# Moving small sums, scalings and a column sum between engines in a two-layer attention kernel, with the whole program in a new order

## The chip, the cores and the metric

The kernel runs on one core of a Trainium2 chip. The time is device microseconds of one execution, the median of several. Products run on TensorE (PE, its weight loads PEld), elementwise work on VectorE (DVE), ScalarE (ACT) and GpSimd (POOL); SyncE (SP) issues nearly all transfers.

## The reference

There are 256 positions of 1024 numbers, in f32, and two layers. Every layer is normalised, shifted, scaled and gated by sums over a conditioning vector `c`:

```
c_act = silu(c)
for layer in range(2):
    ada = c_act @ w_ada[layer] + b_ada[layer]     # 1024 -> 3072
    shift, scale, gate = split(ada, 3)
    h = rms_norm(x, norm_g[layer]) * (1 + scale) + shift
    x = x + gate * mixer(h)
x = rms_norm(x, ...)
```

Layer 0's mixer projects `h` to two groups of heads, A (8 heads, a window of 128 with sinks) and B (8 heads, three branches: compressed, selected, window), multiplies their outputs by `silu` of further projections, and projects back to 1024. Layer 1's mixer has 16 heads; at 256 positions it is causal attention.

## The kernel before, in words

Big products are made of rounded halves. `split` makes `hi`, the f32 number rounded to TensorE's fast format (a cast on ScalarE, `whi`), and `lo`, what is left of it (a difference on VectorE, `wlo`); `mm3` then runs three products, hi·hi, hi·lo and lo·hi. `hhi` and `hlo` are such halves of a layer's input `h`, `ghi` and `glo` those of the gated attention output.

The sums over `c` take three forms. `start_sums` makes layer 0's shift and scale for 2, 2, 2 and 2 columns of 128 (`START`), four sums side by side in one bank (`ps_m`), partly as products with `cz` (the vector `c_act`, one column repeated 32 times) and, in the later groups, partly as a running sum `acc` on VectorE that a product with `ones` then adds over the partitions; the weights lie in buffers that are free so early (`qT`, `gate`, `late`). Its first group has no running sum. `ada_jobs` and `ada_wide` make the later sums, among them layer 1's shift and scale: weight tiles of two rows of 128 go to VectorE, each row one `SCALAR_TENSOR_TENSOR acc<-raw,cz,acc`, save the last `SS_PE` tiles, which `ada_shift_scale` gives to TensorE as products `ps_m<-raw,cz`, 32 columns of weights by 256. `ada_gate` makes a layer's gate: the running sum `acc` is added over the partitions by a matrix of ones, in f32, or, where `GATE_R` says so, as `hi` and `lo` with a rounded matrix of ones (`ones_r`).

`attn_four` does the softmax of four heads for layer 0: scores, maximum (`mn`, VectorE), exponential (ScalarE), then each score tile is scaled by its reciprocal sum `rc`, transposed on TensorE (`ps_pt<-ta,late`) and copied out by ScalarE. Query rows come in two halves: t=0 has tiles of 128x128, t=1 of 128x256. `ON_ACT` says which scalings run on ScalarE.

Nothing runs in the order of the code. Each operation is recorded in a plan, and `ORDER`, a list of some 3,000 operation numbers, says in which order they are issued; it sets the order on all engines and of the transfers, which stand in one queue. So every row of the profile has the same line, 244, and is told by its tiles: `raw` are weights as loaded, `t` scratch tiles, `xs` the residual, `parts` the sums of squares, `late` and `bigA` score tiles, `shs` the finished shift and scale. `WARM` products of ones run ahead of the first data. At the layer boundary the last quarter of layer 0's output (`ps_s` in the rows below) is gated (`t<-ps_s,gate`) and added to `xs`; `xs` is normalised, transposed (`ps_pj<-ta,t`, `ps_o<-ta,t`), scaled and shifted (`t<-ps_pj,shs`), and rounded (`hhi`).

Of the kernel before, what the change touches and what calls it, by code (L numbers as in the profile page):

```python
# [24 lines left out]
GATE_R = (0, 1)  # L25
HV = 4
SS_PE = {0: 0, 4: 2}
SPL = (1024, 1024, 512, 512)
LAST = ((("a", 0, 384), ("v", 384, 1024)), (("a", 0, 192), ("a", 192, 384), ("f", 768, 1024), ("v", 384, 768)))
ON_ACT = ((0, 0, 1), (0, 1, 1), (1, 0, 1), (1, 1, 1))  # L30
# [225 lines left out]
def tile_trunk(  # L256
# [23 lines left out]
    plan = Plan(tc.nc)  # L280
# [433 lines left out]
    def start_sums(g, n, d, w):  # L714
# [10 lines left out]
        for q in range(4):  # L725
# [3 lines left out]
            if d:  # L729
                tq.insert(len(tq) - 1, (ones[:, 0:32], av[:, s_, cs]))  # L730
            terms.append(tq)
        ids = []
        for m in range(max(len(tq) for tq in terms)):
            for q, tq in enumerate(terms):
                if m < len(tq):
                    ids.append(T.matmul(
# [649 lines left out]
```

## Time and profile before

| | before |
|---|---|
| median of 3 runs | 294.93 us (294.6 to 295.61) |
| profiled run | 295.04 us |
| its span, first to last instruction | 293.33 us |
| granted TensorE clock, mean | 0.995 |
| transfers | 71.72 MB, 245 GB/s over the span |

In the rows of the timeline and the groups stand the engine, the line, the operation, `out<-in` by tile names, the shape and the count. In the groups the two numbers behind the bar are busy microseconds and mean nanoseconds of one, and behind the second bar the idle time of the engine just before them. In the timeline the first two numbers are start and length. Products of f32 leave two records each, products of rounded halves one.

### The profile page before, as it was taken

The numbers are of one execution on the slowest core, as the hardware profiler recorded it, in microseconds if no ns is written. First come the engines' busy times: TensorE is split into PE (matmuls) and PEld (weight loads), VectorE is DVE, ScalarE is ACT, GpSimd is POOL, SyncE is SP. The second block draws the span as 40 slices with busy tenths as digits, with TensorE's granted clock in tenths as the row PEclk, the third lists the DMA queues.
The fourth block names the chain that finished last, engine by engine and source line by source line (L and its number), as shares of the span: only waits on it lengthen the run. The fifth ranks groups of instructions, "written<-read, shape, count | busy, mean of one in ns | idle before, by whom it ended". The sixth has DMA issues, their size and how long they took to land.

```text
span 293.3 us, 6197 instructions
## 1 busy us (share of the span) xinstructions
PE 285.4 (97%) x2293; PEld 246.6 (84%) x2293; DVE 252.8 (86%) x629; ACT 188.5 (64%) x480; POOL 8.1 (3%) x33
## 2 busy tenths in 40 slices
PE   8999999999999999999999999999999999999991
PEld 8888788897897888777767899998899999887891
DVE  0497797999999999999889759779978999899884
ACT  4456256895998899994457863366658368584531
POOL 3000000000000000000020000000000000000021
PEclk9999999999999999999999999999999999999998
DMA  7999999999969942769986954569489709502003
GB/s 262 381 365 380 384 380 349 344 349 322 389 233 359 351 147 74 249 234 332 333 256 206 349 167 135 191 242 283 146 258 291 244 0 335 205 36 72 1 3 142
DMA packets 48431, 71.72 MB, mean 245 GB/s; under 512 B 2490, under 2 KB 33938, under 8 KB 48402
## 3 DMA queue, kind: packets, MB, share of 16 engines
q1 hardware_dynamic: 47906, 70.93, 70.6%
q8 instruction: 18, 0.29, 0.4%
q10 hardware_dynamic: 496, 0.41, 0.4%
q14 instruction: 11, 0.09, 0.1%
HBM read 70.28 MB, written 1.05 MB: 243 GB/s over the span
## 4 chain that ended last, share of the span: by engine, by line
PE 82%; DMA 11%; DVE 1%; ACT 1%; issue 1%; POOL 1%; POOLq 0%; DVEq 0%; ACTq 0%
PE ps_pj L244 53%; PE ps_s L244 10%; PE ps_o L244 7%; PE ps_pt L244 7%; PE ps_m L244 5%; DMA gate<-in_w_ada_dram 3%; DMA late<-in_w_ada_dram 3%; DMA raw<-in_w_in_even_dram 3%; DMA qT<-in_w_ada_dram 2%; DMA xs<-in_x_dram 1%; DVE wlo L244 1%; ACT t L244 1%; ACT whi L244 1%; POOL parts L244 1%; DVE t L244 0%
## 5 line engine op out<-in xcount | busy, mean ns | idle before, releaser
L244 ACT CAST whi<-raw 128x512 fp32r<-128x512 f32 (+2 forms) x116 | 71.8, 658 | 27.1 <-PE ps_pj L244 16.5
L244 DVE TENSOR_TENSOR wlo<-raw,whi 128x512 fp32r<-128x512 f32 (+2 forms) x100 | 71.3, 740 | 7.3 <-ACT whi L244 6.6
L244 PE MATMUL ps_pj<-hlo,whi 128*128 128x256 f32 x256 | 70.0, 288 | 0.0
L244 PE MATMUL ps_pj<-hhi,whi 128*128 128x256 f32 x256 | 69.9, 289 | 0.0
L244 PE MATMUL ps_pj<-hhi,wlo 128*128 128x256 f32 x256 | 68.3, 284 | 0.0
L244 PEld LDWEIGHTS ps_pj<-hhi,whi 128*128 128x128 f32 x256 | 46.7, 188 | 1.6 <-issue 0.7
L244 PEld LDWEIGHTS ps_pj<-hlo,whi 128*128 128x128 f32 x256 | 47.1, 189 | 0.8 <-issue 0.7
L244 PEld LDWEIGHTS ps_pj<-hhi,wlo 128*128 128x128 f32 x256 | 46.7, 189 | 0.3
L244 ACT ACTIVATE late<-late,mn 128x128 f32<-128x128 f32 (+1 forms) x58 | 26.0, 450 | 9.2 <-DVE mn L244 9.1
L244 DVE SCALAR_TENSOR_TENSOR acc<-raw,cz,acc 128x1024 f32<-128x1024 f32 x24 | 30.6, 1276 | 0.1
L244 PE MATMUL ps_pj<-whi,hlo 128*128 128x512 f32 (+2 forms) x72 | 25.6, 373 | 0.0
L244 PE MATMUL ps_pj<-wlo,hhi 128*128 128x512 f32 (+2 forms) x72 | 25.5, 372 | 0.0
L244 DVE SCALAR_TENSOR_TENSOR wlo<-raw,whi 128x512 fp32r<-128x512 f32 x32 | 21.1, 686 | 4.5 <-ACT whi L244 4.4
L244 PE MATMUL ps_pj<-whi,hhi 128*128 128x512 f32 (+2 forms) x72 | 24.8, 373 | 0.0
L244 PE MATMUL ps_pj<-wlo,ghi 128*128 128x512 f32 (+1 forms) x56 | 20.6, 371 | 0.0
L244 PE MATMUL ps_pj<-whi,ghi 128*128 128x512 f32 (+1 forms) x56 | 20.6, 371 | 0.0
L244 PE MATMUL ps_pj<-whi,glo 128*128 128x512 f32 (+1 forms) x56 | 20.4, 367 | 0.0
L244 PE MATMUL ps_pt<-ta,late 128*128 128x128 f32 x87 | 19.6, 275 | 0.0
L244 ACT COPY late<-ps_pt 128x384 f32<-128x384 f32 (+1 forms) x29 | 14.0, 483 | 7.9 <-PE ps_pt L244 7.6
L244 PEld LDWEIGHTS ps_pj<-whi,hhi 128*128 128x128 f32 x72 | 13.4, 188 | 2.5 <-ACT hhi L244 0.7
L244 PEld LDWEIGHTS ps_pj<-whi,hlo 128*128 128x128 f32 x72 | 13.6, 188 | 2.0 <-issue 0.2
L244 PEld LDWEIGHTS ps_pj<-wlo,hhi 128*128 128x128 f32 x72 | 13.4, 189 | 1.6
(243 smaller groups left out, 591.0 us busy)
## 6 DMA issues: line engine op xcount, KB each, us to landing
raw<-in_w_in_odd_dram SPq DMA_DIRECT2D x16, 1024.0 KB, 5.7
raw<-in_w_ada_dram SPq DMA_DIRECT2D x8, 1024.0 KB, 8.3
raw<-in_w_ada_dram SPq DMA_DIRECT2D x16, 512.0 KB, 6.3
raw<-in_w_in_even_dram SPq DMA_DIRECT2D x5, 1024.0 KB, 7.9
raw<-in_w_in_even_dram SPq DMA_DIRECT2D x7, 652.0 KB, 7.6
late<-in_w_ada_dram SPq DMA_DIRECT2D x16, 256.0 KB, 6.8
raw<-in_w_out_even_dram SPq DMA_DIRECT2D x4, 1024.0 KB, 5.8
raw<-in_w_out_odd_dram SPq DMA_DIRECT2D x4, 1024.0 KB, 8.7
```

Source lines behind the costliest of these rows:

```text
L244: self.ops.append(dict(key=eng.key, deps=deps, fn=lambda: getattr(real, name)(*args, **kw)))
```

## The change

Four constants or loops change, and the order list.

```
-GATE_R = (0, 1)
+GATE_R = (1, 1)
-SS_PE = {0: 0, 4: 2}
+SS_PE = {0: 0, 4: 1}
-ON_ACT = ((0, 0, 1), (0, 1, 1), (1, 0, 1), (1, 1, 1))
+ON_ACT = tuple((n, i, t) for n in range(2) for i in range(2) for t in range(2))
...
         ids = []
-        for m in range(max(len(tq) for tq in terms)):
-            for q, tq in enumerate(terms):
-                if m < len(tq):
+        size = 4 if d else 2
+        for o in range(0, 4, size):
+            for m in range(max(len(tq) for tq in terms)):
+                for q in range(o, o + size):
+                    tq = terms[q]
+                    if m >= len(tq):
+                        continue
                     ids.append(T.matmul(
...
-        for o in range(0, len(ids), 4):
-            plan.group(ids[o : o + 4])
+        for o in range(0, len(ids), size):
+            plan.group(ids[o : o + size])
...
 ORDER = [int(i) for i in """
-5 0 45 4 9 685 2 3 6 10 37 7 1 85 11 40 38 35 86 12 87 13 14 15 16 17 70 18 88 19 89 20 71 21 72 22 55 23 46 41 39 42 47
+0 4 2 3 1 5 44 45 9 6 35 37 10 7 42 85 11 86 12 87 13 14 15 16 70 88 48 17 49 8 71 18 89 50 55 36 72 90 41 52 46 73 91
...
```

Layer 0's gate is summed as rounded halves too (a cast, a difference and four products in place of two f32 products). In layer 1's second half of shift and scale one weight tile instead of two stays on TensorE; the other goes to the running sum. All of layer 0's scalings stand on ScalarE, 24 of 128x128 more than before. The first sums of layer 0 run the two shift sums to their end and then the two scale sums, instead of four side by side. The order list is new throughout; it has 3,000 operations instead of 3,002.

TensorE at the start of the program, before (`ones` are the products ahead of the data, `crow` and `rows` transposes of `c` and of small vectors, `t_91` and `t_89` transposes of the input, and `qT` the weights of the first shift and scale sums):

```order
L244 MATMUL ps_o_68<-ones 128x128 x15
L244 MATMUL ps_pt_85<-ta,crow 128x8
L244 MATMUL ps_o_68<-ones 128x128 x5
L244 MATMUL ps_pj_95<-ta,t_91 128x128
...
L244 MATMUL ps_s_93<-ta,t_89 128x128 x3
L244 MATMUL ps_m_107<-qT_98,cz 32x128 x2
L244 MATMUL ps_m_107<-qT_100,cz 32x128 x2
L244 MATMUL ps_m_107<-qT_98,cz 32x128 x2
L244 MATMUL ps_m_107<-qT_100,cz 32x128 x2
```

And now:

```order
L244 MATMUL ps_o_68<-ones 128x128 x8
L244 MATMUL ps_pt_85<-ta,crow 128x8
L244 MATMUL ps_o_68<-ones 128x128 x2
L244 MATMUL ps_pt_85<-ta,rows 128x24
L244 MATMUL ps_o_68<-ones 128x128 x5
L244 MATMUL ps_pj_95<-ta,t_91 128x128
L244 MATMUL ps_pj_94<-ta,t_91 128x128
L244 MATMUL ps_pj_95<-ta,t_91 128x128
L244 MATMUL ps_m_107<-qT_98,cz 32x128 x4
```

The transposes of `c` and of the small vectors stand ahead of fewer ones-products, and the first sums stand between the transposes of the input, two side by side.

TensorE at the layer boundary, before: the last product of layer 0's output, four transposes of layer 1's input, the sums of layer 1's shift and scale, and layer 1's first product (`whi,hhi`).

```order
L244 MATMUL ps_s_93<-whi_111,glo 128x512
L244 MATMUL ps_pj_96<-ta,t_88 128x128 x4
L244 MATMUL ps_o_68<-ta,t_88 128x128
L244 MATMUL ps_m_107<-acc_106,ones 32x256 x4
L244 MATMUL ps_m_107<-raw_105,cz 32x256 x8
L244 MATMUL ps_m_107<-raw_103,cz 32x256 x8
L244 MATMUL ps_pj_94<-whi_112,hhi 128x512
```

And now:

```order
L244 MATMUL ps_s_93<-whi_112,glo 128x512
L244 MATMUL ps_pj_96<-ta,t_88 128x128 x4
L244 MATMUL ps_m_107<-acc_106,ones 32x256 x4
L244 MATMUL ps_m_107<-raw_103,cz 32x256 x8
L244 MATMUL ps_o_68<-ta,t_88 128x128 x2
L244 MATMUL ps_pj_94<-whi_113,hhi 128x512
```

Eight products of the sums are gone, and one transpose more stands ahead of layer 1's first product.

ScalarE in layer 0's attention, before (the first scalings by `rc`, between exponentials `late,den<-late,mn` and `es`, and copies out of the banks):

```order
L244 ACTIVATE late,den_127<-late,mn_124 128x128
L244 COPY qT_99<-ps_pt_85 128x2x128
L244 ACTIVATE late<-late,rc_130 128x256
L244 ACTIVATE h_140<-ps_m_107 128x128
L244 ACTIVATE es_134<-mn_124,snk 128x2
L244 ACTIVATE late,den_127<-late,mn_124 128x128
L244 ACTIVATE late,den_127<-late,mn_124 128x256
L244 ACTIVATE h_140<-h_140 128x128
L244 ACTIVATE late<-late,rc_130 128x256
```

And now:

```order
L244 ACTIVATE late,den_127<-late,mn_124 128x128
L244 ACTIVATE late<-late,rc_130 128x128
L244 ACTIVATE late<-late,rc_130 128x256
L244 COPY qT_99<-ps_pt_85 128x2x128
L244 ACTIVATE late<-late,rc_130 128x256 x2
L244 ACTIVATE h_140<-ps_m_107 128x128
L244 ACTIVATE late<-late,rc_130 128x128
L244 ACTIVATE late<-late,rc_130 128x256
L244 ACTIVATE late<-late,rc_130 128x128
```

The scalings of 128x128 stand beside those of 128x256. The cast of the gate's sum, `whi_112<-acc_106`, is placed in the same stretch, further down.

230 rows, old and new, of the table ORDER are left out of this document.

## The prediction

> **What bounds the kernel now.** I read the head of the profile's page first: busy shares, then the shares of the chain that ended last.
>
> ```profile
> PE 285.4 (97%) x2293; PEld 246.6 (84%) x2293; DVE 252.8 (86%) x629; ACT 188.5 (64%) x480; POOL 8.1 (3%) x33
> PE 82%; DMA 11%; DVE 1%; ACT 1%; issue 1%; POOL 1%; POOLq 0%; DVEq 0%; ACTq 0%
> ```
>
> TensorE is on the chain for 82% of the span, transfers for 11%. Where they change places is in the chain in order of time (start, length, what) and in TensorE's own timeline.
>
> ```profile
> 0.80 3.35 DMA xs<-in_x_dram
> 4.16 7.62 DMA gate<-in_w_ada_dram
> 11.79 7.51 DMA late<-in_w_ada_dram
> 19.32 7.42 DMA raw<-in_w_in_even_dram
> 26.75 6.09 DMA qT<-in_w_ada_dram
> ...
> 31.82 0.58 PE L244 MATMUL ps_pj<-whi,hhi 128*128 128x408 f32 x2
> 32.89 0.64 PE L244 MATMUL ps_m<-qT,cz 128*32 128x128 f32 x16 [0.50 <-DMA qT<-in_w_ada_dram]
> ```
>
> Up to 32.89 us an unbroken row of transfers sets the time: the third group of layer 0's shift and scale sums cannot start before its weights land at 26.75 + 6.09 = 32.84. TensorE is out of work half a microsecond earlier. From then on, look at whole stretches (columns: us, then busy time and instructions of PE, PEld, DVE, ACT, POOL, the granted clock, DMA share).
>
> ```profile
> core 0: us, PE busy (x) PEld busy (x) DVE busy (x) ACT busy (x) POOL busy (x), PEclk, DMA share, GB/s
> 14.74:32.89 18.15, 17.65 (x127) 14.65 (x125) 15.76 (x32) 9.24 (x21) 0.00 (x0) 1.00 1.07 373
> 70.00:139.00 69.00, 69.00 (x600) 55.05 (x597) 68.71 (x216) 59.43 (x178) 0.00 (x0) 1.00 0.76 268
> 139.00:150.56 11.56, 11.56 (x50) 8.88 (x50) 9.37 (x18) 5.64 (x10) 1.18 (x3) 1.00 0.98 335
> 160.00:287.05 127.05, 127.05 (x1019) 115.45 (x1016) 110.38 (x256) 75.11 (x182) 1.75 (x4) 1.00 0.52 176
> 287.05:293.33 6.28, 0.00 (x1) 0.00 (x0) 1.92 (x6) 0.80 (x2) 0.55 (x1) 0.77 0.37 136
> ```
>
> The first row has the only pause, 0.50 us, and its transfers are at their limit. In the next three TensorE is busy without a break. That is layer 0's attention (70 to 139), its output projection, and layer 1. In the projection 50 products of 512 columns take 11.56 us, 0.231 each, the same step as elsewhere, so nothing is hidden in "busy" there. The last row is a tail of 6.28 us that no product enters. So what counts is TensorE's own work after 32.89, the pause before it, and whether VectorE (68.71 of 69.00 us!) and ScalarE (59.43) still keep up in the attention.
>
> **The change part by part.** *Opening: pairs and other order.* The same transfers stand ahead of the third group's weights, save a few tiny ones that change places, so the pin near 32.84 stays. In the new order, counted row by row by columns, 0.44 us more product work stands ahead of the third group's sums and 0.87 us more ahead of those behind them. Work put into the pause is work not done later: at least 0 (if the pin moves later by as much), at most the pause: 0.50 by the row, or 0.70 if the last two products of 408 columns, from 31.82, take 0.231 × 408/512 = 0.184 each and end at 32.19. I take 0.5 saved, near the 0.44. Fewer ones-products ahead of the constants and sums in pairs instead of fours lie before 14.74; each sum is still two products of the same width in one bank, and the copy behind them waits for all.
>
> ```profile
> 11.05 1.18 PE L244 MATMUL ps_m<-qT,cz 128*32 128x128 f32 x34
> 13.10 0.27 ACT L244 COPY asb<-ps_m 128x128 f32<-128x128 f32 x1 [3.83 <-PE ps_m L244]
> ```
>
> If all of those sums came twice as slowly (1.18 us more), 0.7 would be covered by the pause and 0.5 would show. I cost them at nothing.
>
> *Layer 0's gate by rounded halves.* TensorE loses two f32 products of 512 columns (two records each) and gets four rounded ones. The timeline gives the old ones with their followers; the groups by shape give the rest.
>
> ```profile
> 100.85 1.02 PE L244 MATMUL ps_m<-acc,ones 128*128 128x512 f32 x2
> 101.80 1.08 PE L244 MATMUL ps_o<-bigA,vb 128*64 128x256 f32 x9
> ...
> 103.74 1.02 PE L244 MATMUL ps_m<-acc,ones 128*128 128x512 f32 x2
> 104.70 0.93 PE L244 MATMUL ps_s<-late,qT 64*128 64x128 f32 x8
> ...
> L244 PE MATMUL ps_m<-acc,ones 128*128 128x512 f32 x4 | 2.0, 592 | 0.0
> L244 PE MATMUL ps_m<-whi,ones_r 128*128 128x512 f32 x2 | 0.8, 392 | 0.0
> L244 PE MATMUL ps_m<-wlo,ones_r 128*128 128x512 f32 x2 | 0.8, 392 | 0.0
> L244 ACT CAST whi<-acc 128x1024 fp32r<-128x1024 f32 x1 | 1.0, 1049 | 0.0
> L244 DVE TENSOR_TENSOR wlo<-acc,whi 128x1024 fp32r<-128x1024 f32 x1 | 1.2, 1218 | 0.0
> ```
>
> Each old product holds TensorE 0.95 us (100.85 to 101.80, 103.74 to 104.70), together 1.91; four at 0.231 are 0.92. That saves 0.98. The groups' busy times, which count overlaps between neighbours, give 2.0 − 1.6 = 0.4. I take 0.9, since a follower's start tells more than a modelled end. For it ScalarE gets a cast of 1.05 and VectorE a difference of 1.22; they stand in the attention, where TensorE has other products.
>
> *Layer 1's sums.* A second weight tile of two goes to VectorE. TensorE loses half of 32 records, VectorE gets two sums of 1024 columns.
>
> ```profile
> L244 PE MATMUL ps_m<-raw,cz 128*32 128x256 f32 x32 | 1.9, 379 | 0.0
> L244 DVE SCALAR_TENSOR_TENSOR acc<-raw,cz,acc 128x1024 f32<-128x1024 f32 x24 | 30.6, 1276 | 0.1
> ...
> 150.33 0.39 PE L244 MATMUL ps_s<-whi,glo 128*128 128x512 f32 x1
> 151.71 1.91 PE L244 MATMUL ps_m<-raw,cz 128*32 128x256 f32 x32
> 153.55 0.50 PE L244 MATMUL ps_pj<-whi,hhi 128*128 128x512 f32 x1
> ...
> 151.02 0.68 DVE L244 TENSOR_TENSOR t<-ps_s,gate 128x512 f32<-128x512 f32 x1
> 151.94 0.68 DVE L244 TENSOR_TENSOR xs<-xs,t 128x512 f32<-128x512 f32 x1
> ...
> 153.03 0.41 ACT L244 CAST hhi<-t 128x256 fp32r<-128x256 f32 x1 [1.26 <-DVE t L244]
> ```
>
> That is 1.91/2 = 0.95 us less of TensorE and 2 × 1.276 = 2.55 more of VectorE. But look where the sums stand: they fill the layer boundary. While they run (151.71 to 153.55), VectorE gates the last part of layer 0's output (151.02), adds it to the residual (151.94) and makes two columns of layer 1's input, and ScalarE rounds them (153.03 to 153.44); only then can layer 1's first product start, 0.11 us later, at 153.55. That chain stays as it is in the new order. With 0.95 of the cover gone TensorE waits about as long; one or two transposes pulled in ahead are all that it keeps. I take 0.1 saved; the ends are 0 and 0.95.
>
> *Scalings to ScalarE.* Layer 0 has 24 scalings of 128x128 on VectorE, which go to ScalarE. The groups:
>
> ```profile
> L244 DVE TENSOR_SCALAR late<-late,rc 128x128 f32<-128x128 f32 x29 | 7.8, 277 | 0.0
> L244 ACT ACTIVATE late<-late,rc 128x256 f32<-128x256 f32 x15 | 7.4, 507 | 0.2
> L244 ACT ACTIVATE late<-late,mn 128x128 f32<-128x128 f32 x29 | 11.5, 396 | 3.5 <-DVE mn L244 3.5
> ```
>
> VectorE loses 24 × 0.277 = 6.6 us. For a scaling of 128 columns on ScalarE there is no row: it lies between 0.277 (VectorE's for the same tile) and 0.507 (ScalarE's of twice the width); nearest is ScalarE's exponential of the same tile, 0.396, so 24 × 0.396 = 9.5, ends 6.6 and 12.2. ScalarE's idle time in that stretch is 69.00 − 59.43 = 9.57, of which the gate's cast takes 1.05. So it fits only just: 59.43 + 1.05 + 9.5 = 70.0 against TensorE's 69.00 − 0.9 = 68.1. Records that follow each other on one engine overlap in part, so the sum of durations is too high, and I take nothing lost; the other case is a rival. The Trainium skill, "ScalarE: Activation LUTs", section "What ACT_TABLE_LOAD costs", gives 186 ns and 0.833 per column, 93 more for a pointer operand, 93 less back to back: an estimate of 0.29 us by that page, or 7.1 in all, by which ScalarE would have 67.6 us of work and fit.
>
> *The tail.* One normalising of the first half of the rows moves behind the last sum of squares on VectorE, into its wait.
>
> ```profile
> 285.84 0.55 DVE L244 TENSOR_SCALAR t<-xs,parts 128x640 f32<-128x640 f32 x1
> 288.96 0.42 DVE L244 TENSOR_SCALAR t<-xs,parts 128x384 f32<-128x384 f32 x1 [0.67 <-POOL parts L244]
> ```
>
> It takes 0.55 and the wait is 0.67, so it fits; between 0.15 saved and 0.3 lost, I take 0.
>
> The sum: −0.5 − 0.9 − 0.1 = −1.5 us against the profiled run of 295.04 us (span 293.33 and 1.71 around it), which lies 0.11 above the median of the runs, 294.93. Predicted 293.5.
>
> **The rivals.** *A, the sum above*, 292.7 to 294.6: nothing of the opening and 0.4 for the gate give −0.4, the whole pause and 0.95 of the boundary −2.3 with some loss elsewhere.
>
> *B, VectorE sets the attention's pace.* It is busy 68.71 of 69.00 there. TensorE's busy time is built of modelled ends, and its weight loads are busy only 55.05. For it: no engine but these has so little idle time. Against it: the exponentials waited for VectorE's maxima only 3.5 us in all, and TensorE shows no gap. VectorE would be freed of 6.6 − 1.2 − 2.5 = 2.9 us if both extra sums stand there; with the opening that is 295.04 − 2.9 − 0.5 = 291.6, and 292.6 if ScalarE stops it halfway. The Trainium skill, "Perfetto Trace Analysis", section "Identifying the Most-Contended Engine", judges TensorE's headroom by weight loads and not by busy products; by that rule TensorE at 80% has room and VectorE, at nearly 100%, is the bound. Whether the trace bears it out, this profile alone does not show; the even step of 0.231 in the projection speaks against it there.
>
> *C, ScalarE becomes the bound and eats the gain.* With 70.0 us of work as above the attention ends 1.0 later instead of 0.9 earlier: −0.5 − 0.1 + 1.0 = +0.4, 295.4; with half of the overlap 294.7. Within 0.3%.
>
> *D, slower: transposes wait for scalings in ScalarE's queue.* Each of the six calls scales for two groups of heads, 12 in all; the transposes behind a group now wait for scalings that stand between exponentials, casts of weights and copies out of the banks on one engine. If TensorE loses 0.22 us in each (half of one 0.396-us instruction), 2.7 in all, the result is 293.5 + 2.7 = 296.2. From 0.2 a group on it is slower by over 0.3%. For it: ScalarE has nothing spare by the sum of durations, and the four scalings of a group would be in one file instead of shared by two engines. Against it: the order lays other products between, since TensorE has no gap today although half of the scalings stand on ScalarE already.
>
> **How the numbers follow.** A 0.50, B 0.12, C 0.20, D 0.18. What a measurement of this kernel can tell from no change is 0.3%, 0.88 us, so the bound is 294.05 below and 295.8 above. A ends partly inside it (0.06 of its 0.50); C mostly (0.17, the rest split on both sides); D reaches over it with 0.17. Faster 0.44 + 0.12 + 0.01 = 0.57, the same 0.06 + 0.17 + 0.01 = 0.24, slower 0.02 + 0.17 = 0.19. The range takes in A and C whole, the upper half of B and the lower part of D: 292.0 to 296.0. A's own is 292.7 to 294.6.
>
> **What the changed profile would show.** The wait for the third group's weights shorter than 0.2 us (opening right). Four ones-products of about 0.39 in the attention in place of four of 0.59 (gate right). A wait of TensorE for the rounded input of about 0.8 us at the layer boundary (layer 1's sums worth little; without a wait they are worth 0.95). In the attention VectorE's idle time up by two or three microseconds with TensorE still unbroken (A), TensorE's instructions in fewer microseconds by far more than 0.9 (B), ScalarE near 100% with TensorE waiting for its copies or scalings (C, in many small pieces behind scalings D). I would be wrong above all if a stretch that I cost at nothing, layer 1 from 160 on or the tail, moved by a microsecond, since the whole program stands in another order.

## The result, and the profile after

The changed kernel takes 297.23 us (296.97 to 297.33) against 294.88 before (294.60 to 295.61): ratio 1.0074, 95% interval 1.0055 to 1.0094. (The ratio isn't that of the two medians, so the two can differ by 0.1%.) It is slower by 0.7%, where 293.5 and a gain were forecast. The profiled execution took 297.20 us, 2.16 more than the one before. First the busy shares and the chain that ended last, then TensorE's waits (us in total, times, longest).

```profile
PE 284.9 (96%) x2277; PEld 245.8 (83%) x2277; DVE 251.7 (85%) x608; ACT 194.8 (66%) x505; POOL 8.9 (3%) x33
PE 90%; DMA 4%; DVE 2%; issue 1%; SPq 1%; ACT 0%; ACTq 0%; POOLq 0%; POOL 0%; DVEq 0%
PE ps_pj L244 <- ACT whi L244: 1.8, 1, 1.8
PE ps_pt L244 <- DMA rows<-in_b_ada_dram: 0.5, 1, 0.5
```

TensorE is busy for 0.5 us less, but two waits of the opening are in the list, 1.8 and 0.5 us long; a third of 0.3 stands in the rows below. Of stretches (busy time of PE, PEld, DVE, ACT, POOL, granted clock, DMA share, GB/s) the first two rows are of before, the others of after.

```profile
28.00:36.00 8.00, 7.50 (x74) 6.17 (x73) 6.17 (x14) 2.30 (x7) 0.00 (x0) 1.00 1.07 378
36.00:40.00 4.00, 4.00 (x23) 3.50 (x22) 4.00 (x10) 2.90 (x7) 0.00 (x0) 1.00 1.07 366
...
28.00:36.00 8.00, 7.69 (x74) 6.22 (x73) 5.68 (x12) 2.58 (x6) 0.00 (x0) 1.00 0.86 251
36.00:40.00 4.00, 2.19 (x10) 1.33 (x8) 1.99 (x8) 1.88 (x4) 0.00 (x0) 1.00 1.00 363
70.00:139.00 69.00, 69.00 (x609) 56.83 (x609) 67.46 (x194) 67.09 (x208) 0.63 (x3) 1.00 0.80 286
288.85:295.40 6.55, 0.00 (x0) 0.00 (x0) 2.19 (x6) 0.80 (x2) 0.79 (x1) 0.70 0.44 161
```

Between 28 and 36 us the transfers moved 251 GB/s, where they had moved 378. TensorE pays for it in 36 to 40, where it is busy for 2.19 of 4.00 us. The timeline of TensorE and ScalarE and the chain (its lines hold start, length, what) say what was late:

```profile
34.56 0.43 PE L244 MATMUL ps_m<-gate,cz 128*32 128x128 f32 x8 [0.31 <-DMA gate<-in_w_ada_dram]
39.39 0.98 PE L244 MATMUL ps_pj<-whi,hhi 128*128 128x512 f32 x3 [1.81 <-ACT whi L244]
38.72 1.66 ACT L244 CAST whi<-raw 128x512 fp32r<-128x512 f32 x3 [1.76 <-DMA raw<-in_w_in_even_dram]
31.42 7.23 DMA raw<-in_w_in_even_dram
```

The third group's weights come at 34.5 instead of 32.84. The next projection weights, issued at 31.42, land at 38.65; ScalarE casts them at once, and TensorE starts on them at 39.39. The wait for `whi` is thus a wait for a transfer. SyncE's queue in both kernels, issues in order of time (start, length; a run of issues to one tile is one row), before first:

```profile
23.10 4.03 SPq L244 DMA_DIRECT2D qT<-in_w_ada_dram  x4
27.53 0.37 SPq L244 DMA_DIRECT2D gate<-in_w_ada_dram  x1
...
20.38 0.28 SPq L244 DMA_DIRECT2D srow<-in_a_sinks_dram  x1
21.87 1.13 SPq L244 DMA_DIRECT2D qT<-in_w_ada_dram  x2
23.29 0.30 SPq L244 DMA_DIRECT2D rows<-in_norm_g_dram  x1
24.95 4.12 SPq L244 DMA_DIRECT2D qT<-in_w_ada_dram  x4
29.12 0.46 SPq L244 DMA_DIRECT2D rows<-in_cmp_pe_k_dram  x1
29.63 0.93 SPq L244 DMA_DIRECT2D gate<-in_w_ada_dram  x2
32.36 0.43 SPq L244 DMA_DIRECT2D rows<-in_cmp_pe_v_dram  x1
```

In the new order five small transfers (8 KB of `b_ada`, 32 bytes of `a_sinks`, 4 KB of `norm_g`, 8 KB each of `cmp_pe_k` and `cmp_pe_v`), which stood behind 40 us before, stand between the large ones (`b_ada`'s, at 8.83, isn't in the rows), and the last `gate` tile is issued at about 30.1 instead of 27.53. Four of the five stand ahead of it; `cmp_pe_v` is issued behind it.

The account: between each product and the next I count TensorE's idle time (a modelled end is taken 0.165 us earlier, as it shows in an unbroken run). In 0 to 40 us it rose from 2.21 to 4.93 (1.0 of that before 10 us, 1.84 in 30 to 40, 0.16 less between), in 150 to 160 from 0.31 to 1.05, elsewhere from 7.56 to 7.61: +3.51. The last product ends 1.80 later (288.85 against 287.05), so its products took 1.71 less. The tail is 0.27 longer and what lies around the span 0.09: 1.80 + 0.27 + 0.09 = 2.16. By the same count, from one product's start to the next without the idle time, gate and layer 1's sums took 1.65 less. The 52 ones-products, as many as before, took 1.14 less, since TensorE came to its full pace earlier in this profile (more on that under the tail). The first sums in pairs took 0.54 more, and the rest 0.5 more, which I can't place. So that the 1.71 is near the saving of gate and sums is in part chance.

### The profile page after: what moved, and what is told of

It is laid out like the page before. It is cut to its first block, busy times and chain, and to the rows that moved or that the text cites. A ratio compares the mean times of both kernels' runs of the same rounds, so it can differ in the third digit from the quotient of the medians.

```text
span 295.4 us, 6137 instructions
## 1 busy us (share of the span) xinstructions
PE 284.9 (96%) x2277; PEld 245.8 (83%) x2277; DVE 251.7 (85%) x608; ACT 194.8 (66%) x505; POOL 8.9 (3%) x33
## 3 DMA queue, kind: packets, MB, share of 16 engines
HBM read 70.28 MB, written 1.05 MB: 241 GB/s over the span
## 4 chain that ended last, share of the span: by engine, by line
PE 90%; DMA 4%; DVE 2%; issue 1%; SPq 1%; ACT 0%; ACTq 0%; POOLq 0%; POOL 0%; DVEq 0%
PE ps_pj L244 58%; PE ps_s L244 10%; PE ps_o L244 9%; PE ps_pt L244 7%; PE ps_m L244 5%; DMA raw<-in_w_in_even_dram 2%; DMA rows<-in_b_ada_dram 1%; SPq L244 1%; DVE xs L244 1%; DVE t L244 1%; ACTq L244 0%; POOLq L1385 0%; ACT whi L244 0%; DVE wlo L244 0%; ACT t L244 0%
## 5 line engine op out<-in xcount | busy, mean ns | idle before, releaser
L244 PE MATMUL ps_pj<-hhi,whi 128*128 128x256 f32 x256 | 71.2, 294 | 0.0
L244 DVE SCALAR_TENSOR_TENSOR acc<-raw,cz,acc 128x1024 f32<-128x1024 f32 x26 | 33.3, 1280 | 0.2
L244 PE MATMUL ps_pj<-whi,hhi 128*128 128x512 f32 (+2 forms) x72 | 25.7, 377 | 1.8 <-ACT whi L244 1.8
L244 ACT COPY asb<-ps_m 128x128 f32<-128x128 f32 (+1 forms) x7 | 2.2, 310 | 19.6 <-PE ps_m L244 19.6
```

The costliest lines, as they stand in the source:

```text
L244: self.ops.append(dict(key=eng.key, deps=deps, fn=lambda: getattr(real, name)(*args, **kw)))
```

## The experiments

All were timed in five rounds against the kernel before. The theory: the small transfers in the opening cost the time, and gate and sums bring what was forecast. The rivals: ScalarE or VectorE became the bound, the early pause of the ones-products, or the tail.

### The small transfers

**Only they, in the kernel before.** The other engines keep their order. SyncE's:

```
 DMA raw_104<-in_w_in_even_dram 128x384
 DMA qT_98<-in_w_ada_dram 128x2x256
+DMA rows<-in_norm_g_dram 8x128
 DMA gate<-in_w_ada_dram 128x2x256
 DMA qT_99<-in_w_ada_dram 128x2x256 x2
+DMA rows<-in_cmp_pe_k_dram 16x128
...
 DMA tb<-in_tbl_b_dram 128x1056
-DMA rows<-in_b_ada_dram 16x128
-DMA rows<-in_norm_g_dram 8x128
```

> The kernel before, with nothing changed but that the same five small transfers stand where the changed kernel has them, between the opening's big ones. Theory Q: the rate at 28 to 36 us falls to 215 to 275 GB/s, the third group's weights land 1 to 2 us later, and the time rises by 1.2 to 2.3 us, to 296.1 to 297.2. Rivals B and P: the places of the small ones do not matter; 294.9 within 0.4.

Measured: 298.42, ratio 1.0097 (1.0077 to 1.0117). Its stretches:

```profile
28.00:34.00 6.00, 5.62 (x57) 4.48 (x55) 5.42 (x10) 1.56 (x4) 0.00 (x0) 1.00 0.79 229
34.00:36.00 2.00, 0.59 (x9) 0.22 (x9) 0.00 (x0) 0.00 (x0) 0.00 (x0) 0.88 0.97 359
36.00:40.00 4.00, 4.00 (x14) 3.38 (x14) 2.52 (x8) 2.46 (x6) 0.00 (x0) 0.63 1.02 352
```

28 KB in the wrong place cost 3.3 us. The transfers fall to 229 GB/s, TensorE waits 1.5 us for the same weights, and then its granted clock is 0.63 over 4 us. By the count above, idle time up to 40 us rises by 2.1 us here while the last product ends 3.2 later; the slow clock is the likely rest, and the changed kernel's profile has no such stretch. This alone turns the kernel before into one that is slower than the changed kernel.

**One of the five.** Only `cmp_pe_k` is moved.

> The kernel before with one small transfer alone (a position table, 8 KB) moved ahead, between the weights of the third group; five moved cost 3.3 us. Theory Q, each takes one of eight places for about the 6 to 7 us that a transfer is under way, so it costs the bytes of one place, 0.25 MB, 0.7 us at 375 GB/s: the third group's weights land 0.5 to 0.8 us later and the time rises by 0.3 to 0.8 us. If it is not the places but the sheer handling of an issue, 0.45 us of SyncE's time that is not short there: no change.

Measured: 295.19, ratio 1.0012 (1.0003 to 1.0021), no wait at 32 us. That is less than a fifth of 3.3, so the cost doesn't add up one by one. Whether it hangs on how many fall into one stretch, or on which, no run tells; the others were not moved one by one.

**Put back in the changed kernel,** all in a row behind the loads of the next weights, or one by one between large transfers:

```
+DMA rows<-in_cmp_pe_v_dram 16x128
 DMA raw_104<-in_w_in_even_dram 128x8x256
+DMA rows<-in_cmp_pe_k_dram 16x128
 DMA tb<-in_tbl_b_dram 128x1056
+DMA rows<-in_b_ada_dram 16x128
 DMA w2v<-in_cmp_w_v_dram 128x2x64
```

> The changed kernel, but its five small transfers (b_ada, the sinks, norm_g and two position tables, 0.03 to 8 KB each) stand again behind the opening's big ones, as in the kernel before; the one transpose that reads them and its copy stand later too. Theory Q (the small transfers take places in a queue that keeps eight transfers in flight, so the bytes in flight and the rate fall): the rate at 28 to 36 us is back at 350 to 400 GB/s, TensorE's wait at 37.4 for the row of weights falls from 1.97 us to below 0.5, and the time falls by 1.5 to 2.3 us, to 294.9 to 295.7. Rival B (the order of the big transfers does it: the second part of a weight row stands ahead of the first): the rate is back, but a wait of over 1 us stays; the time falls by less than 0.8. Rival P (TensorE's own new order uses up its work too early): the wait stays whatever the queue does; no change, 297.2.

> The changed kernel with its five small transfers behind the opening's big ones and one by one between transfers of 0.25 to 1 MB, as the kernel before has them (in the run with all five in a row the rate fell to 146 GB/s at 46 to 48 us, and TensorE then waited 0.65 us at 59 and 0.45 at 73.5). Theory Q: no wait of the opening over 0.3 us is left, the rate stays over 320 GB/s from 28 to 50 us, and the time is about that of the kernel before: 295.0 within 0.4. If the two waits have other causes: 295.9, as with all five in a row.

Measured: in a row 295.92, ratio 1.0030 (1.0013 to 1.0046); spread 295.58, ratio 1.0020 (1.0004 to 1.0036). Here is the spread kernel's stretch, and then the place where the row of five stands in the other:

```profile
28.00:36.00 8.00, 8.00 (x78) 6.78 (x77) 6.08 (x13) 2.51 (x6) 0.00 (x0) 1.00 1.07 381
...
46.00:48.00 2.00, 2.00 (x12) 1.68 (x11) 1.90 (x7) 1.72 (x5) 0.00 (x0) 1.00 0.59 146
```

The rate is back at 381 and TensorE's wait in 30 to 40 us is gone. Of the 2.3 us lost, 1.3 to 1.7 were the small transfers. Five in a row only move the hole, to 46 us (146 GB/s), where less hangs on it.

**What does a small transfer take?** In the issue order each transfer waits on one of eight semaphores (counters that tell of a landing), in turn, whichever engine issues it, so eight are in flight at most. Theory: a small one holds one of eight places until it lands. Rival: it costs SyncE's issue time. First the same bytes of the third group, in the kernel before, in 16 transfers instead of 8:

```
-            Y.dma_start(w[k], src[:, k, 0:2, P * g : P * (g + n)])
+            if g == 4:
+                for s_ in range(2):
+                    Y.dma_start(w[k][:, s_], src[:, k, s_, P * g : P * (g + n)])
```

> The kernel before with the third group's eight weight transfers of 0.25 MB each split into two of 0.125 MB, 16 in the same places of the queue; the same bytes in the same order. Theory that eight transfers are in flight and the bytes in flight set the rate: 8 x 0.125 MB in flight, the rate between 22 and 34 us falls below 320 GB/s, the third group's last weights land 0.5 to 2 us later, and the time rises by 0.5 to 2 us (ratio 1.002 to 1.007). Rival, a small transfer costs by its latency or its destination and not by the place that it takes: rate and time unchanged (ratio 0.999 to 1.001).

Measured: 298.22, ratio 1.0110 (1.0097 to 1.0123), more than either theory gave.

```profile
26.00:30.00 4.00, 4.00 (x25) 3.60 (x25) 3.81 (x10) 3.51 (x8) 0.00 (x0) 1.00 0.69 220
26.92 4.56 SPq L245 DMA_DIRECT2D qT<-in_w_ada_dram  x8
```

No byte was added, so it is the number of transfers that costs. But 8 issues in 4.56 us, one every 0.57, are 0.131 MB / 0.57 = 230 GB/s, so from 27 us on this run also fits the rival. Two runs take issues from SyncE:

```
-    load_rows(Y, 1)
-    Y.dma_start(srow[0:1, :], a_sinks)
+    load_rows(A, 1)
+    A.dma_start(srow[0:1, :], a_sinks)
```

(and the two `cmp_pe` tables; in the changed kernel), and in the kernel with halves `(Y, A)[s_].dma_start(...)`.

> The changed kernel with its five small transfers issued by ScalarE at the same numbers of the order, instead of by SyncE. In the order the transfers of both engines share the same eight semaphores in turn, so on this theory a small transfer takes a place wherever it is issued: the rate between 28 and 36 us stays below 300 GB/s, TensorE still waits about 2 us in all between 34 and 40 us, and the time stays at 296.8 to 298.5 (ScalarE waiting for a place can make it worse). Rival, the time that SyncE needs to issue (0.45 to 0.6 us apiece) is the cost: five issues fewer on SyncE, the rate is back above 340 GB/s, and the time falls to 295.3 to 296.

> The kernel before with the third group's weights in 16 transfers of 0.125 MB, the second half of each pair issued by ScalarE. Theory of the eight shared places: bytes in flight are as few as with all of them on SyncE, the rate between 26 and 34 us stays below 300 GB/s and the time near 298.2 or above (ScalarE's casts wait behind its issues). Rival, SyncE's issue time bounds the rate there (0.125 MB in 0.47 us is 279 GB/s, which is what the run with all halves on SyncE shows): with two issuing engines the rate is back above 340 GB/s and the time nearer 295 to 296.

Measured: small ones on ScalarE 296.00, ratio 1.0024 (1.0006 to 1.0042), halves on two engines 299.50, ratio 1.0142 (1.0119 to 1.0166). The first two rows are of the former; then the latter's stretch, its SyncE's next issue, and ScalarE's transfer issued at 26.72 (KB, us to landing).

```profile
28.00:32.00 4.00, 4.00 (x25) 3.68 (x24) 3.96 (x9) 2.25 (x5) 0.00 (x0) 1.00 1.02 329
32.00:36.00 4.00, 4.00 (x55) 3.05 (x54) 2.33 (x7) 0.56 (x3) 0.00 (x0) 1.00 0.96 313
...
30.00:36.00 6.00, 5.93 (x58) 4.60 (x56) 5.34 (x10) 1.72 (x4) 0.00 (x0) 1.00 0.72 202
31.52 1.28 SPq L245 DMA_DIRECT2D qT<-in_w_ada_dram  x3
qT<-in_w_ada_dram ACTq DMA_DIRECT2D x1, 128.0 KB, 4.8
```

Neither theory holds alone. For the small ones the rival was right on the time and half right on the rate (329 and 313): with five issues fewer on SyncE 1.2 us come back, though the places taken are as many. The Trainium skill ("DMA: Bandwidth & Descriptors", section "Issuing engines are not separate DMA queues") says that issuing from several engines saves only the sequencer's time to issue, usually small; here that time was worth 1.2 us. In the other run the places show: after its issue at 27.16 SyncE issues nothing until 31.52, and 26.72 + 4.8 = 31.5 is when the transfer whose place the next one takes has landed. So a transfer costs both, an issue of 0.3 to 0.6 us and a place until it lands. Their shares in the changed kernel stay open; moving issues also shifted them in time by a microsecond or so. In its profile both occur: SyncE waits for landings up to 24.95 and 27.02, and from 28.44 to 31.42 the chain that ended last is one issue behind the other, `cmp_pe_k`'s among them with 0.46.

### The rest of the opening, and the tail

**Tail put back in the spread kernel; then four ones-products ahead of the second early transpose as well ("mended").**

```
 MATMUL ps_pt_85<-ta,crow 128x8
-MATMUL ps_o_68<-ones 128x128 x2
+MATMUL ps_o_68<-ones 128x128 x6
 MATMUL ps_pt_85<-ta,rows 128x24
-MATMUL ps_o_68<-ones 128x128 x5
+MATMUL ps_o_68<-ones 128x128
...
+TENSOR_SCALAR t_89<-xs,parts 128x640
 TENSOR_TENSOR xs<-xs,bigA 128x256
...
-TENSOR_SCALAR t_89<-xs,parts 128x640
```

> The changed kernel with the five small transfers spread one by one among the large ones and the end's order put back; the four products with the row of ones stay where the change put them. It stands between the run with the small transfers spread alone (295.58) and the one with the ones-products moved as well (294.86). If the last 0.7 us between those two was the pause at 5.5 to 6.2 us before the second early transpose, this one stays at about 295.3 (only the end's 0.27 us comes back). If it was the end's order, it comes to about 294.9.

> As the run with the small transfers spread, with two more places of the changed order put back: four products of ones ahead of the second early transpose (it waits for a small transfer at 5.5 to 6.15 us), and in the tail the normalising of 640 columns ahead of the last sum of squares instead of behind it. Theory: the tail loses the 0.27 us that it had gained (GpSimd's last power takes 0.55 again instead of 0.79), and without the pause TensorE is at its full pace by 7 us in every run, so the runs scatter less: 294.7 within 0.4. If neither place matters: the same as with the transfers spread alone.

Measured: spread and tail 295.38, ratio 0.9999 (0.9975 to 1.0023), too wide to give the last 0.7 us to either; mended 294.86, ratio 0.9991 (0.9983 to 1.0000). The early pause is no constant: the transpose waited 0.5 us in the changed kernel, 0.9 in the one with small transfers on ScalarE, and not at all in the profile of spread and tail. Its transfer (`rows`, ScalarE's queue) lands at different times. Another thing varies there: the moment at which TensorE comes to its full pace. The same ten ones-products in the changed kernel, then in spread and tail:

```profile
6.29 1.38 PE L244 MATMUL ps_o<-ones 128*128 128x128 f32 x10
6.50 2.50 PE L244 MATMUL ps_o<-ones 128*128 128x128 f32 x10
```

From start to start one takes 0.21 us at first and 0.11 later. The change comes near 5 us in the changed kernel's profile, near 7 before and in mended, and past 10 in spread and tail. That profiled execution took 296.03, and the kernel's runs scatter from 294.19 to 296.76, mended's from 294.23 to 295.16. That the moved ones-products prevent the late change isn't shown, with one profile of each. Mended is the best version found: 0.2 us below before at the median, with an interval that ends at no change. The forecast gain of 1.5 is not there even without the opening's fault.

**The opening in its old order** (its first 685 operations, sums in fours, the rest as changed), and **mended with sums in fours**:

```
-        size = 4 if d else 2
+        size = 4
```

> The changed kernel from the attention on (gate, layer 1's sums, scalings, its order), but the opening in full as in the kernel before: its first 685 operations in the old order on all engines and in the queue, first sums in fours, and the tail put back. Theory: the whole loss beyond small terms is the new opening, so this shows what the rest is worth: 0.4 us better than the mended kernel, 294.4 within 0.3, TensorE waiting at 32 for the third group and not again before 100. If the rest of the new order loses too: 294.9 or more.

> The mended kernel with the first sums of layer 0 four side by side again instead of in pairs; the two scale sums' products stand with the first two, ahead of the transposes. Reckoned before as nothing: 294.9 within 0.4. If the early sums of the pair help the opening: 0.3 to 1 us slower, since TensorE then waits for the weights of the scale at 8 to 9 us with the transposes behind it.

Measured: old opening 295.84, ratio 1.0029 (1.0016 to 1.0042), where 294.4 was expected; at the seam TensorE waited twice for ScalarE (0.9 in all). Without that it would be near 294.9, an estimate, so here too the rest of the change brings no gain over the kernel before (294.98 in these rounds). Mended in fours 299.71, ratio 1.0157 (1.0138 to 1.0175): placed as early as the pairs, they wait 3.0 us for weights, and the clock falls.

```profile
PE ps_m L244 <- DMA qT<-in_w_ada_dram: 3.0, 1, 3.0
12.00:16.00 4.00, 4.00 (x40) 3.24 (x38) 0.69 (x1) 0.00 (x0) 0.00 (x0) 0.74 1.04 402
```

The pairs make the early place possible, but they cost work. The rows before (the sums begin at 11.05, as the prediction shows), then now:

```profile
12.94 0.33 PE L244 MATMUL ps_s<-ta,t 128*128 128x128 f32 x1
...
8.11 0.63 PE L244 MATMUL ps_m<-qT,cz 128*32 128x128 f32 x8
8.67 0.33 PE L244 MATMUL ps_pj<-ta,t 128*128 128x128 f32 x1
10.91 1.10 PE L244 MATMUL ps_m<-qT,cz 128*32 128x128 f32 x32
12.78 0.33 PE L244 MATMUL ps_s<-ta,t 128*128 128x128 f32 x1
```

In fours they hold TensorE from 11.05 to 12.94, 1.89 us; in pairs from 8.11 to 8.67 and from 10.91 to 12.78, 2.43 us: 0.54 more.

### Gate, scalings and layer 1's sums

**Parts taken out of the mended kernel.** The gate in f32, or the scalings back on VectorE, or two tiles on TensorE:

```
-GATE_R = (1, 1)
+GATE_R = (0, 1)
```

```
-ON_ACT = tuple((n, i, t) for n in range(2) for i in range(2) for t in range(2))
+ON_ACT = ((0, 0, 1), (0, 1, 1), (1, 0, 1), (1, 1, 1))
```

```
-SS_PE = {0: 0, 4: 1}
+SS_PE = {0: 0, 4: 2}
```

> The mended kernel with layer 0's gate by two f32 products again, placed soon after the running sum so that its buffer is free as early as with the cast. If the rounded halves save TensorE 0.9 us in the attention, as reckoned: 0.9 us slower than the mended kernel, 295.6. If ScalarE or VectorE are the bound there: no slower, or up to 1.2 us faster.

> The mended kernel (small transfers spread, four products of ones moved, tail put back; 294.86) with the 24 scalings of 128x128 on VectorE again, each right behind its reciprocal. In the mended kernel TensorE waits 0.48 us at 136 for a VectorE operation that follows ScalarE's work, and the changed kernel's scalings took ScalarE 0.40 us each, 9.6 in all. If ScalarE has become the bound there (rival C): faster, 294.0 to 294.5. If VectorE needs the relief to take the gate's difference and the two extra sums (2.4 + 2.6 us more work for it in this stretch): slower, by 1 to 4 us, with TensorE waiting for VectorE's maxima and differences.

> The mended kernel with two weight tiles of layer 1's sums on TensorE again, as before the change (VectorE 2.55 us less, TensorE 0.95 more at the layer boundary). As reckoned, the boundary's wait for the gated output (0.45 and 0.16 us there) is filled by these products and the time is 0.1 to 0.2 us longer, no more than can be told. If TensorE's work counts there in full: 0.95 longer. If VectorE's relief counts: up to 1 us shorter.

Measured: gate 296.62, ratio 1.0054 (1.0042 to 1.0067), 1.8 above mended; scalings 299.87, ratio 1.0158 (1.0145 to 1.0171), 5.0 above; two tiles 305.41, ratio 1.0367 (1.0348 to 1.0387). The last is confounded: the tile's buffer is held longer, a layer-1 weight load comes late, and TensorE waits 6.2 us for layer 1's rounded input, so it prices nothing. In the run with scalings on VectorE the longest wait behind the program's start is for VectorE:

```profile
PE ps_s L244 <- DVE wlo L244: 1.1, 1, 1.1
```

In this order VectorE can't scale beside the gate's difference and the two sums without holding TensorE up: its relief pays for the other two parts.

**The same parts alone in the kernel before.**

> The kernel before with nothing changed but the 24 scalings of late, bigA and so on, issued on ScalarE at the places where VectorE's stood; about 24 x 0.4 us leave VectorE. Theory that TensorE sets the pace of the kernel before and VectorE has just enough slack there: no change, ratio 0.998 to 1.003. Rival, VectorE bounds the attention: ratio 0.985 to 0.995 (gain of 1.5 to 4 us, the sum of the waits for VectorE in the attention). Rival, ScalarE can't take them without a delay of the transposes: ratio above 1.003.

> The kernel before with layer 0's gate by rounded halves and nothing else; the cast and difference stand where the running sum is done, the products some 40 places behind them. If TensorE's work is what counts in the attention: 0.9 us faster, 294.0 within 0.3. If VectorE (68.7 of 69.0 us busy there) is the bound: no gain, or up to 1.2 us slower.

> The kernel before with nothing changed but layer 1's sums of shift and scale: one tile instead of two on TensorE, the other share on VectorE. TensorE has about 0.95 us less work, VectorE about 2.5 us more, in its tight stretch. If TensorE's work alone counts: 294.0 to 294.5 (ratio 0.997 to 0.999). If VectorE has no slack there without the scalings moved: ratio 1.003 to 1.015, with waits of TensorE for VectorE between 100 and 150 us.

> The changed kernel with layer 0's gate again by two f32 products (no cast, no difference, four rounded products fewer). If the gate's saving on TensorE is real there, as reckoned (0.9 us): 298.1 within 0.3. If ScalarE or VectorE are the bound in the attention, so that their 1.05 and 1.22 us less pay for it: no change or faster, 296.5 to 297.2.

Measured: scalings alone 298.53, ratio 1.0120 (1.0107 to 1.0133); gate alone 301.12, ratio 1.0188 (1.0165 to 1.0211); one tile alone 307.21, ratio 1.0410 (1.0397 to 1.0424); and the changed kernel with only its gate in f32 at the rounded products' places 301.98, ratio 1.0222 (1.0189 to 1.0254). In the last the running sum is held longer and VectorE's next sums wait; with one tile alone that tile's transfer stands where TensorE's did, and VectorE waits 9.1 us for it. Both are faults of my placing and price nothing. The other two show their place, scalings first, then the gate:

```profile
110.00:120.00 10.00, 8.57 (x64) 6.80 (x64) 9.16 (x26) 10.00 (x23) 0.00 (x0) 1.00 0.16 55
PE ps_pt L244 <- ACT t L244: 1.4, 2, 1.1
...
PE ps_pt L245 <- DVE t L245: 2.5, 1, 2.5
99.97 1.22 DVE L245 TENSOR_TENSOR wlo<-acc,whi 128x1024 fp32r<-128x1024 f32 x1 [1.29 <-ACT whi L245]
108.00:112.00 4.00, 4.00 (x19) 3.72 (x18) 3.33 (x9) 2.63 (x9) 0.00 (x0) 0.50 0.18 70
```

Scalings put on ScalarE at the places where VectorE's stood fill ScalarE to 10.00 of 10 us, and transposes wait for it. In the gate's run VectorE waits 1.29 us for ScalarE's cast of the sum and then makes the difference in 1.22; the 2.51 together are as long as TensorE's wait for VectorE's next results, and then the clock is at 0.50. So neither part can stand at these places of the old order; others weren't tried.

## Why the prediction was wrong, step by step

**Opening: the step that failed.** "The same transfers stand ahead of the third group's weights, save a few tiny ones that change places, so the pin near 32.84 stays." I weighed the small transfers by bytes, though their place in the queue was on record in the order. The weights behind them landed 1.7 us later, and the term forecast at −0.5 came out at +2.7 (4.93 − 2.21 of idle time). That is 3.2 of the 3.7 us between forecast and time. The small transfers account for 1.3 to 1.7 of it, by the runs that put them back. What the rest hangs on isn't shown; two terms that I had costed at nothing stand in the opening too, the pause before the second early transpose (0.5 us here) and the pairs (0.54 us of work).

Even with the pin back, the 0.5 wasn't there to gain. In the mended kernel the third group starts without a wait at 33.39 instead of 32.89: the pause is filled, but 0.54 us of what fills it is the pairs' own extra work.

**Gate: right.** Four products in place of four records, each 0.23 from start to start:

```profile
114.79 0.40 PE L244 MATMUL ps_m<-wlo,ones_r 128*128 128x512 f32 x1
115.02 0.28 PE L244 MATMUL ps_pj<-hhi,wlo 128*128 128x256 f32 x1
```

Gate and sums together take 1.65 us off TensorE's products, where 0.98 + 0.95 were counted. The run with the f32 gate agrees in sign, but its +1.8 is twice the gate's work, and what the rest hangs on wasn't settled.

**Layer 1's sums: right.** The saving becomes a wait, as forecast (0.85): TensorE's idle time in 150 to 160 us rises by 0.74, and 0.1 to 0.2 of the saving is left.

```profile
152.08 0.40 PE L244 MATMUL ps_s<-whi,glo 128*128 128x512 f32 x1
152.76 0.66 PE L244 MATMUL ps_pj<-ta,t 128*128 128x128 f32 x4 [0.28 <-DVE t L244]
```

**Scalings: right in size; the sum of durations was too high.** The duration was forecast at 0.396 and is 0.398, but one follows the other after 0.30:

```profile
L244 ACT ACTIVATE late<-late,rc 128x128 f32<-128x128 f32 x15 | 6.0, 398 | 0.0
90.18 0.41 ACT L244 ACTIVATE late<-late,rc 128x128 f32<-128x128 f32 x1
90.48 0.39 ACT L244 ACTIVATE bigA<-bigA,rc 128x128 f32<-128x128 f32 x1
```

So 24 take 7.2 us of ScalarE and not 9.5, an estimate; its busy time in 70 to 139 us grew by 7.66 with the cast of 1.05, which leaves 6.6. The estimate of 0.29 by the Trainium skill ("ScalarE: Activation LUTs", section "What ACT_TABLE_LOAD costs") agrees with the 0.30. ScalarE is busy 67.09 of 69.00 us in 70 to 139, and TensorE shows no wait for a scaling: rivals C and D did not occur in the changed kernel. The slower end came by another way than D.

**Rival B** isn't borne out: 24 scalings off VectorE alone made the kernel slower, not faster, and in the changed kernel TensorE's idle time outside the opening and the boundary stays at 7.6. But ScalarE was full in the former run, so VectorE's relief has no price by itself. By the Trainium skill's rule on the most-contended engine ("Perfetto Trace Analysis", section "Identifying the Most-Contended Engine") VectorE was the one to relieve; here the time went the other way.

**Tail: inside its bounds.** The normalising of 640 columns fits into the wait by its own 0.55, but GpSimd's power beside it takes 0.79 instead of 0.55, and the last normalising waits for it. After first, then before:

```profile
289.86 0.55 DVE L244 TENSOR_SCALAR t<-xs,parts 128x640 f32<-128x640 f32 x1
290.02 0.79 POOL L244 TENSOR_TENSOR parts<-parts,expo 128x1 f32<-128x1 f32 x1 [1.50 <-DVE parts L244]
...
288.38 0.55 POOL L244 TENSOR_TENSOR parts<-parts,expo 128x1 f32<-128x1 f32 x1 [1.93 <-DVE parts L244]
```

The tail grew by 0.27, within the bounds given (0.15 saved to 0.3 lost); I had taken 0. Layer 1 was costed at nothing, and it cost nothing.

Why the mended kernel gains only 0.2, by the same count: its last product ends 0.13 us earlier than before, with 0.8 more idle time (0.73 at the boundary, 0.55 in 130 to 140 us, 0.37 less in the opening, 0.1 less elsewhere). So its products took only 0.95 less: of the 1.65 saved by gate and sums the pairs took 0.54 back. What stays open is the longer wait in 130 to 140 us and the last 0.2 of the products.

## What to carry to other kernels

Where a stage hangs on transfers, count the transfers that stand ahead of its last one, not the bytes: a table of 4 to 8 KB among 0.25 MB tiles costs an issue and a place. Put small tables behind the pinned weights, one by one between large transfers, or on another engine's queue. And work moved between engines has no price apart from its order: the scalings and the gate, each put alone into an order made for the other division, lost 3.5 and 6 us.

## What the runs showed of the hardware

The granted clock fell after some waits of TensorE, by the mean over 4 us behind them: to 0.63 after one of 1.5 us, to 0.50 after one of 2.5, to 0.74 after one of 3.0. After the changed kernel's own wait of 1.8 us it stayed at 1.00. The Trainium skill ("TensorE: Matmul & The Clock Gate", section "Why this matters for your kernels") tells one to avoid idle gaps above about 3 us; here shorter ones were enough in some runs, so a wait of 1.5 us has to be priced with the slow 4 us that may follow it. At the start a 128x128 product of ones takes 0.21 us from start to start and later 0.11; the change came between 4 and 7.3 us in eighteen of the twenty profiles and past 10 in two. And a halving of transfer size from 0.25 to 0.125 MB took the rate from 358 to 220 GB/s for 4 us, at the same bytes.
